# Row parts for three tiles at a time on VectorE, and another pace of the row fetches before and after the first gates

## The chip, the core and the metric

The kernel runs on one core of a Trainium2 chip, as one launch. The metric is device time in microseconds of that launch, lower is better. The core has a matrix engine (PE in the rows, TensorE), a vector engine (DVE), a scalar engine (ACT), GpSimd (POOL), a queue engine (SP) and 16 DMA engines that all transfers share.

## What is computed

A decoder trunk of two layers over 256 positions of width 1024. Each layer has a mixer and then an expert-retrieval stage, `peer`, with 16,384 experts:

```
def peer(xn, w_q, sub_keys, u, v):
    q = (t @ w_q).reshape(n_tok, 8, 2, 128)            # 8 heads, two half keys
    sc = einsum('thpd,hpnd->thpn', q, sub_keys)         # scores against 2 x 128 keys
    ... top 16 of each half, top 16 of their sums -> expert numbers e, gate g = softmax
    hid = gelu(einsum('td,thkd->thk', t, u[e]))         # one dot product an expert
    return einsum('thk,thkd->td', g * hid, v[e])
```

All tensors are float32. The whole is: mixer 0 (attention and retention), peer 0, mixer 1 (a short convolution), peer 1, a last norm.

## The kernel before

**Two ways through the experts.** Of the 256 tokens, 96 fetch the rows of `u` and `v` that they chose, and the other 160 (`TD`) are done densely: every expert's `u` row and `v` row is multiplied with all 160 tokens, and the gates (mostly zero) pick. For the 96, one *row step* fetches 128 rows of 1024 floats (0.524 MB, one indirect DMA that GpSimd issues, L866) and reduces them on DVE, L876 for `u` and L891 for `v`. There are 192 row steps a layer: 96 of `u`, then 96 of `v`. Six buffers (`grow`, `rows`) hold fetched rows; a fetch is issued when the step six before it is done.

**The u stage** (`for i in range(NK)`, 128 tiles of `u`, each 128x1024 floats, 0.524 MB, sent by SP). `dense_u` multiplies tile i into a PSUM tile `hid` (8 products, L1235), ACT applies Gelu into row i of `HG`. Meanwhile DVE works off `pump`, a list of top-16 searches. When it is empty, tile 58, the gates start: `onehots(g)` makes for four tokens two one-hot matrices in the buffer `KO` (8 ACT steps, one DVE step L1190), and `slot`, called twice a tile, adds `rate` to a credit and, at 1, emits `g_mm` (4 products, L1198), `onehots(g+2)` and `g_put`, which multiplies the gates into `HG` (L1208). There are 40 such groups. `ga.rate` says how many row steps are emitted for each tile: 0.6 up to tile 7, 0.88 from there to the gates, then so many that `UPTO[l]` steps are done by tile 117.

**The v stage** (128 tiles of `v`, sent by SP and ACT in turn, eight buffers `raw`). 33 tiles are multiplied as they are (L1324). The 95 *split* tiles (`SPL`: every odd one and every fourth, so that there is one whole tile, then three split ones) are cut into a high part `vhi` (ACT, L1246) and a low part `vlo` (DVE, L1253). The 160 numbers of `HG` that belong to the tile are cut likewise: `hs` holds the high part (ACT, L1300) and the rest (GpSimd, L1305), and `hb` a bf16 copy (ACT, L1301). PE then does eight products of `vhi` with both halves of `hs` (L1328) and eight of `vlo` with `hb` (L1330). At tile i, the parts of tile i+3 are made, the rests of tile i+2, and the DMA of tile i+7 is issued. The other row steps are spread over tiles 2 to 114.

**Order.** Every engine runs its instructions in the order in which the program emits them; a wait holds what is behind it on that engine.

Of the kernel before, what the change touches and what calls it, by code (L numbers as in the profile page):

```python
# [18 lines left out]
P = 128  # L19
# [21 lines left out]
MORE = 4  # L41
GT = 4
SCR = 11 * D
UPTO = (126, 119)
SPL = [i for i in range(NK) if i % 2 or i % 4 == 0 and i > 0]
CODE = 64.0
WHOLE = 1.5 * 2.0 ** 23
# [135 lines left out]
def trunk_kernel(ctx, tc, x, small, cst, mcst, ew_in, ew_out, ow_in, ow_out, wq, keys, pu, pv, pun, gains, out):  # L183
# [33 lines left out]
    KO = pers.tile([P, NPAIR * NK], F32, tag="ko", name="ko")  # L217
# [21 lines left out]
    def nm(s):  # L239
        uid[0] += 1  # L240
        return f"{s}{uid[0]}"
# [250 lines left out]
    class Final(Sums):  # L492


        def __init__(self, xs, g):
            super().__init__()
            self.xs = xs
            self.g = g

        def warm(self):  # L500
# [66 lines left out]
    def split_act(c2, cb, k, src, t, alone=False):  # L567
# [345 lines left out]
    def peer(l, before, norm):  # L913
        with tc.tile_pool(name=nm("hg"), bufs=1) as hp:
# [7 lines left out]
                assert off[0] <= NK * TD  # L922
                return flat[:, o:o + n]

            skT = KO
# [330 lines left out]
            for i in range(NK):  # L1256
                ps = dense_u(i)
                if i == 0:
                    after_first()
                elif early_u:  # L1260
                    fetch(early_u.pop(0))
                if i == NK - 1:
                    gst["rate"] = 1.0
                    while gst["g"] < NG:
                        slot(i)
                T = max(gst["g"], 0) * GT
                if T < TD:
                    act.activation(HG[:, i, T:], ps[:, T:TD], AF.Gelu)  # L1268
                if T > 0:
                    act.activation(ps[:, :T], ps[:, :T], AF.Gelu)  # L1270
                    v.tensor_tensor(HG[:, i, :T], ps[:, :T], HG[:, i, :T], OP.mult)  # L1271
                slot(i + 1)
                if gst["g"] < 0:
                    if i == first_late - 2:
                        pump.flush()
                    if pump.q:
                        pump.run(1.4)
                    else:
                        gst["g"] = 0
                        gst["rate"] = NG / (2.0 * (NK - 8 - i))  # L1280
                        onehots(0)
                        onehots(1)
                ga.rate = (0.6 if i < 8 else 0.88) if gst["g"] < 0 else (UPTO[l] - ga.c) / (NK - CALM - i) if i < NK - CALM else 0.6
                if i < NK - QUIET:
                    ga.step()
                elif i in (NK - QUIET, NK - QUIET + 2):
                    weight_parts(i - NK + QUIET + 1)
            upool.close()
            vpool = ExitStack()
            vp = vpool.enter_context(tc.tile_pool(name=nm("vp"), bufs=3))  # L1290
            OT = XG.rearrange("p q d -> p (q d)")[:, :ND * S].rearrange("p (b t) -> p b t", b=ND)

            assert ga.c >= STEPS
            ga.rate = (ga.TOTAL - ga.c) / (NK - 14.0)
            vo = [acc_tile(b, nm("vo")) for b in range(4)]
            vo += [side_tile(nm("vo")) for _ in range(2)] + [hid_tile(nm("vo")) for _ in range(2)]
            def row_parts(j):
                hsb[j] = hs, hb = [vp.tile([P, 2, TD], F32R, tag="hs", name=nm("hs")),
                                   vp.tile([P, TD], BF16, tag="hb", name=nm("hb"))]
                act.copy(hs[:, 0, :], HG[:, j, :])  # L1300
                act.copy(hb, HG[:, j, :])  # L1301

            def row_rest(j):
                hs = hsb[j][0]
                gp.tensor_tensor(hs[:, 1, :], HG[:, j, :], hs[:, 0, :].bitcast(F32), OP.subtract)  # L1305

            for j in (1, 3):
                row_parts(j)
                row_rest(j)
            for i in range(NK):  # L1310
                j = i + AHEAD
                if 4 <= j and j in SPL:
                    weight_parts(j, False)
                    row_parts(j)
                if 4 <= j - 1 and j - 1 in SPL:
                    weight_rest(j - 1)
                    row_rest(j - 1)
                if i == NK - 8:
                    norm.warm()
                w = st.next()  # L1320
                m = dict(start=i == 0, skip_group_check=True)
                if i not in SPL:
                    for b in range(ND):
                        pe.matmul(vo[b][:, :TD], w[:, b * P:(b + 1) * P], HG[:, i, :], stop=False, **m)  # L1324
                else:
                    hi, lo, (hs, hb) = whi.pop(i), wlo.pop(i), hsb.pop(i)
                    for b in range(ND):
# [25 lines left out]
    with tc.manual_schedule():  # L1353
        norms = [Norm(0)]
        nc.sync.dma_start(G, small)
        nc.sync.dma_start(C[:, :P], cst[:, :P])
        for th in range(2):
            (nc.scalar if th else nc.sync).dma_start(h[:, th, :], x[th])
        nc.sync.dma_start(C[:, P:], cst[:, P:])
        v.memset(Z, 0.0)  # L1360
        act.activation(norms[0].w[:, 0, 6:7], Z[:, 0:1], AF.Sqrt)
        for _ in range(3):
            st._load()
        busy(24)
# [7 lines left out]
        peer(1, a, Final(KO.rearrange("p (a d) -> p a d", a=2), XF.rearrange("p k t -> p (k t)")[:, :D]))  # L1372


# [36 lines left out]
```

## Time and profile before

| | |
|---|---|
| time, median of 3 runs | 1518.8 us (1514.49 to 1521.89) |
| the profiled execution's own time | 1520.15 us |
| its span, first to last instruction | 1518.4 us |
| PE busy | 1461.4 us, 96% |
| DVE, ACT, POOL busy | 1218.0, 812.0, 891.7 us |
| moved by DMA | 533.05 MB, mean 351 GB/s |

By the times at which the engines change lines, the u stage of layer 0 runs from 183.4 to 508.8 us, its v stage to 764.7, the u stage of layer 1 from 919.5 to 1243.9, its v stage to 1505.6. Shares over the whole span mix these stages with the mixers, so the tables by stage below are what is to be read.

### The profile page before, as it was taken

Reading aid. Unit: us, or ns where it says so; the run is one execution under the profiler, and the core shown is the slowest. Engines: PE = TensorE matmul, PEld = TensorE weight load, DVE = VectorE, ACT = ScalarE, POOL = GpSimd, SP = SyncE. Lnnn points to the kernel's source line nnn. Section 1 sums busy time; section 2 is a strip of 40 time slices with the busy share of each in tenths; the row PEclk is TensorE's granted clock in tenths of the full one; section 3 lists DMA queues with packets and bytes.
Section 4 is the critical chain, followed back from the end, with each engine's and each line's share of the span. In section 5 each row is a group of like instructions: output and inputs, shape, how many; then the busy total and the mean of one; then the engine's idle time right before and its main releaser. Section 6 shows DMA issues by size and latency. Waiting matters only on the chain.

```text
span 1518.4 us, 30875 instructions
## 1 busy us (share of the span) xinstructions
PE 1461.4 (96%) x11108; PEld 1364.2 (90%) x11108; DVE 1218.0 (80%) x2406; ACT 812.0 (53%) x2062; POOL 891.7 (59%) x704
## 2 busy tenths in 40 slices
PE   9999999989999999999999999998999999999997
PEld 5667999989999998889989799998999998988896
DVE  5637999868888788888787599995788869888896
ACT  5556512258887455555653462213888845555554
POOL 6754545445554587778535273553565538787763
PEclk9999999999999999999999999999999999999999
DMA  8546899999999999999966498999999999999993
GB/s 314 196 153 207 288 406 409 397 407 409 407 401 409 390 401 409 395 395 393 337 217 198 150 321 335 409 407 397 385 394 393 392 380 392 408 407 400 403 393 141
DMA packets 147577, 533.05 MB, mean 351 GB/s; under 512 B 16992, under 2 KB 17248, under 8 KB 147424
## 3 DMA queue, kind: packets, MB, share of 16 engines
q1 hardware_dynamic: 72144, 258.36, 45.1%
q0 software_dynamic: 56704, 205.07, 34.5%
q10 hardware_dynamic: 18576, 67.64, 11.7%
q8 instruction: 88, 1.44, 0.4%
q14 instruction: 65, 0.53, 0.1%
HBM read 528.34 MB, written 1.05 MB: 349 GB/s over the span
## 4 chain that ended last, share of the span: by engine, by line
PE 50%; DVE 23%; DMA 18%; issue 4%; POOL 3%; ACT 2%; ACTq 0%; SPq 0%; POOLq 0%; DVEq 0%
PE hid L1235 17%; DMA raw<-pv 13%; PE vo L1328 7%; PE G L1198 4%; PE vo L1324 4%; DMA rows<-pun,ig 4%; DVE rows L876 3%; PE vo L1330 3%; PE hid L250 3%; DVE hg L992 2%; DVE hg L998 2%; DVE hg L994 2%; DVE grow L876 2%; PE ea L286 2%; PE ea L285 2%
## 5 line engine op out<-in xcount | busy, mean ns | idle before, releaser
L1235 PE MATMUL hid<-xf,raw 128*128 128x160 f32 x3456 | 489.6, 300 | 0.0
L1235 PEld LDWEIGHTS hid<-xf,raw 128*128 128x128 f32 x3456 | 476.4, 191 | 0.0
L1246 ACT CAST vhi<-raw 128x1024 fp32r<-128x1024 f32 x190 | 198.9, 1047 | 227.5 <-DMA raw<-pv 155.6
L1253 DVE TENSOR_TENSOR vlo<-raw,vhi 128x1024 bf16<-128x1024 f32 x190 | 246.7, 1303 | 88.6 <-ACT vhi L1246 87.6
L1328 PE MATMUL vo<-hs,vhi 128*128 128x320 f32 x1520 | 272.8, 321 | 23.9 <-POOL hs L1305 23.6
L1328 PEld LDWEIGHTS vo<-hs,vhi 128*128 128x128 f32 x1520 | 226.0, 189 | 31.8 <-POOL hs L1305 31.7
L866 POOL DMA_INDIRECT rows<-pv,ig x128 | 177.2, 1384 | 100.6 <-DVE gacc L891 44.5
L1305 POOL TENSOR_TENSOR hs<-hg,hs 128x160 fp32r<-128x160 f32 x190 | 202.4, 1072 | 51.0 <-ACT hs L1300 47.8
L866 POOL DMA_INDIRECT rows<-pun,ig x128 | 153.8, 1202 | 133.2 <-DVE rows L876 71.8
L146 POOL TENSOR_TENSOR lo<-raw,hi 128x1024 bf16<-128x1024 f32 x68 | 163.2, 2415 | 76.8 <-ACT hi L144 73.8
L876 DVE SCALAR_TENSOR_TENSOR rows<-rows,xg 128x1024 f32<-128x1024 f32 x128 | 155.2, 1218 | 31.5 <-DMA rows<-pun,ig 31.4
L1268 ACT ACTIVATE hg<-hid 128x160 f32<-128x160 f32 (+25 forms) x242 | 63.8, 269 | 214.5 <-PE hid L1235 208.8
L891 DVE SCALAR_TENSOR_TENSOR gacc<-rows,ghid,gacc 128x1024 f32<-128x1024 f32 x124 | 171.5, 1383 | 5.8 <-DMA rows<-pv,ig 5.4
L1324 PE MATMUL vo<-hg,raw 128*128 128x160 f32 x1056 | 157.2, 302 | 0.5 <-DVE hg L1271 0.5
L1324 PEld LDWEIGHTS vo<-hg,raw 128*128 128x128 f32 x1056 | 145.5, 190 | 0.8 <-DVE hg L1271 0.8
L1330 PE MATMUL vo<-hb,vlo 128*128 128x160 bf16 x1520 | 139.1, 235 | 0.0
L1189 ACT ACTIVATE ko<-ko,idxT 128x128 f32<-128x128 f32 x320 | 130.8, 481 | 0.0
L866 POOL DMA_INDIRECT grow<-pun,ig x64 | 75.7, 1183 | 87.9 <-DVE grow L876 52.0
L866 POOL DMA_INDIRECT grow<-pv,ig x64 | 86.7, 1355 | 61.0 <-DVE gacc L891 33.1
L1186 ACT ACTIVATE ko<-cst,idxT 128x128 f32<-128x128 f32 x320 | 102.4, 390 | 33.2 <-PE G L1198 33.0
L1330 PEld LDWEIGHTS <-vlo 128*128 128x128 bf16 x1520 | 101.3, 99 | 19.6 <-issue 0.2
L144 ACT CAST hi<-raw 128x1024 fp32r<-128x1024 f32 x100 | 102.5, 1047 | 18.2 <-issue 10.2
(228 smaller groups left out, 2198.9 us busy)
## 6 DMA issues: line engine op xcount, KB each, us to landing
raw<-pu SPq DMA_DIRECT2D x216, 512.0 KB, 7.6
raw<-pv SPq DMA_DIRECT2D x128, 512.0 KB, 7.8
raw<-pv ACTq DMA_DIRECT2D x128, 512.0 KB, 7.8
raw<-wq SPq DMA_DIRECT2D x32, 512.0 KB, 3.9
raw<-ew_in SPq DMA_DIRECT2D x28, 512.0 KB, 4.5
raw<-ow_in SPq DMA_DIRECT2D x24, 512.0 KB, 5.3
hg<-pu SPq DMA_DIRECT2D x22, 512.0 KB, 5.2
raw<-ew_out SPq DMA_DIRECT2D x8, 512.0 KB, 3.2
```

Source lines behind the costliest of these rows:

```text
L146: eng.tensor_tensor(lo, t, hi.bitcast(F32), OP.subtract)
L866: gp.indirect_dma_start(self.row(s_), None, table, bass.IndirectOffsetOnAxis(IG[:, 0, s_ % STEPS:s_ % STEPS + 1].bitcast(U32), 0))
L876: v.scalar_tensor_tensor(r, r, 1.0, XG[:, q % 2, :], op0=OP.mult, op1=OP.mult, accum_out=w)
L891: v.scalar_tensor_tensor(self.acc[q], r, w, self.acc[q], op0=OP.mult, op1=OP.add)
L1189: act.activation(B[:, j], B[:, j], AF.Relu, bias=idxT[:, 2, t:t + 1], scale=idxT[:, 3, t:t + 1])
L1235: pe.matmul(ps[:, :TD], w[k], XF[:, k, :], start=k == 0, stop=k == ND - 1)
L1246: act.copy(whi[j], raw)
L1253: v.tensor_tensor(wlo[j], raw, whi[j].bitcast(F32), OP.subtract)
L1305: gp.tensor_tensor(hs[:, 1, :], HG[:, j, :], hs[:, 0, :].bitcast(F32), OP.subtract)
L1324: pe.matmul(vo[b][:, :TD], w[:, b * P:(b + 1) * P], HG[:, i, :], stop=False, **m)
L1328: pe.matmul(vo[b][:, :2 * TD], hi[:, b * P:(b + 1) * P], hs, stop=i == NK - 1, **m)
L1330: pe.matmul(vo[b][:, :TD], lo[:, b * P:(b + 1) * P], hb, stop=i == NK - 1, **m)
```

## The change

The rest of a row part, `hs[:, 1, :]`, is made by DVE, for a whole run of split tiles (three, at the ends one) in one instruction, and ACT makes the high parts and the bf16 copies of a run in one instruction each. The two halves of the key buffer `KO`, free once the gates are done, hold `hs` in turn. So GpSimd keeps only the row fetches in the v stage. Three tables of numbers change: `UPTO` of layer 1, the row rate ahead of the gates (0.9 for tiles 8 to 45, then 0.6), and the pace of the gates, which begins at a credit of -0.6 and ends two tiles earlier.

```diff
-UPTO = (126, 119)
+UPTO = (126, 122)
...
                         gst["g"] = 0
-                        gst["rate"] = NG / (2.0 * (NK - 8 - i))
+                        gst["rate"] = NG / (2.0 * (NK - 10 - i))
+                        gst["credit"] = -0.6
...
-                ga.rate = (0.6 if i < 8 else 0.88) if gst["g"] < 0 else (UPTO[l] - ga.c) / (NK - CALM - i) if i < NK - CALM else 0.6
+                ga.rate = (0.9 if 8 <= i < 46 else 0.6) if gst["g"] < 0 else (UPTO[l] - ga.c) / (NK - CALM - i) if i < NK - CALM else 0.6
...
+            halves = new_ko(F32R).rearrange("p (a n) -> p a n", a=2)[:, :, :6 * TD]
...
             def row_parts(j):
-                hsb[j] = hs, hb = [vp.tile([P, 2, TD], F32R, tag="hs", name=nm("hs")),
-                                   vp.tile([P, TD], BF16, tag="hb", name=nm("hb"))]
-                act.copy(hs[:, 0, :], HG[:, j, :])
-                act.copy(hb, HG[:, j, :])
-
-            def row_rest(j):
-                hs = hsb[j][0]
-                gp.tensor_tensor(hs[:, 1, :], HG[:, j, :], hs[:, 0, :].bitcast(F32), OP.subtract)
+                n = run_of(j)
+                hs = halves[:, (j + 1) // 4 % 2].rearrange("p (j s t) -> p j s t", j=3, s=2)[:, :n]
+                hb = vp.tile([P, 3, TD], BF16, tag="hb", name=nm("hb"))[:, :n]
+                act.copy(hs[:, :, 0, :], HG[:, j:j + n, :])
+                act.copy(hb, HG[:, j:j + n, :])
...
+            def row_rest():
+                j, n, hs = hsb.pop("rest")
+                v.tensor_tensor(hs[:, :, 1, :], HG[:, j:j + n, :], hs[:, :, 0, :].bitcast(F32), OP.subtract)
...
                 if 4 <= j and j in SPL:
                     weight_parts(j, False)
-                    row_parts(j)
+                    if j - 1 not in SPL:
+                        row_parts(j)
                 if 4 <= j - 1 and j - 1 in SPL:
                     weight_rest(j - 1)
-                    row_rest(j - 1)
+                    if "rest" in hsb:
+                        row_rest()
```

DVE's instructions in layer 0, u stage, around the first one-hots (`ko<-cst,idxT`); the rows L876 (L882) are row steps. Before:

```order
L1103 TENSOR_TENSOR hg_1256<-hg_1256 128x128
L876 SCALAR_TENSOR_TENSOR rows_2048,ghid_1261<-rows_2048,xg 128x1024 x2
L876 SCALAR_TENSOR_TENSOR grow_1257,ghid_1261<-grow_1257,xg 128x1024 x2
L876 SCALAR_TENSOR_TENSOR rows_2048,ghid_1261<-rows_2048,xg 128x1024 x4
L1190 TENSOR_TENSOR ko<-cst,idxT_1265 128x512 x2
L876 SCALAR_TENSOR_TENSOR grow_1257,ghid_1261<-grow_1257,xg 128x1024 x2
L876 SCALAR_TENSOR_TENSOR rows_2048,ghid_1261<-rows_2048,xg 128x1024
L1190 TENSOR_TENSOR ko<-cst,idxT_1265 128x512
```

and after:

```order
L1109 TENSOR_TENSOR hg_1256<-hg_1256 128x128
L882 SCALAR_TENSOR_TENSOR rows_2048,ghid_1261<-rows_2048,xg 128x1024 x2
L882 SCALAR_TENSOR_TENSOR grow_1257,ghid_1261<-grow_1257,xg 128x1024 x2
L882 SCALAR_TENSOR_TENSOR rows_2048,ghid_1261<-rows_2048,xg 128x1024 x2
L1196 TENSOR_TENSOR ko_612<-cst,idxT_1265 128x512 x2
L882 SCALAR_TENSOR_TENSOR rows_2048,ghid_1261<-rows_2048,xg 128x1024 x2
L882 SCALAR_TENSOR_TENSOR grow_1257,ghid_1261<-grow_1257,xg 128x1024 x2
L1196 TENSOR_TENSOR ko_612<-cst,idxT_1265 128x512
```

Two row steps fewer stand ahead of the first two one-hots, and four instead of three between them and the third.

PE at the same place, with the tiles `hid` of the u stage and the first two gate groups `G`. Before:

```order
L1235 MATMUL hid_3089<-xf,raw_2947 128x160 x8
L1235 MATMUL hid_3103<-xf,raw_2961 128x160 x8
L1198 MATMUL G_3113<-ko 128x128 x4
L1235 MATMUL hid_3133<-xf,raw_2975 128x160 x8
L1235 MATMUL hid_3151<-xf,raw_2989 128x160 x4
L1198 MATMUL G_3156<-ko 128x128 x4
```

and after:

```order
L1241 MATMUL hid_3083<-xf,raw_2945 128x160 x8
L1241 MATMUL hid_3097<-xf,raw_2959 128x160 x8
L1241 MATMUL hid_3113<-xf,raw_2973 128x160 x4
L1204 MATMUL G_3118<-ko_612 128x128 x4
L1241 MATMUL hid_3113<-xf,raw_2973 128x160 x4
L1241 MATMUL hid_3145<-xf,raw_2985 128x160 x8
L1204 MATMUL G_3157<-ko_612 128x128 x4
```

The first gate group stands half a u tile later.

DVE in the v stage of layer 0, where `vlo` is the low part of a tile and `gacc` a row step. Before:

```order
L1253 TENSOR_TENSOR vlo_5567<-raw_5460,vhi_5546 128x1024
L891 SCALAR_TENSOR_TENSOR gacc_1259<-rows_2048,ghid_1261,gacc_1259 128x1024
L1253 TENSOR_TENSOR vlo_5620<-raw_5499,vhi_5588 128x1024
L1253 TENSOR_TENSOR vlo_5647<-raw_5528,vhi_5614 128x1024
L891 SCALAR_TENSOR_TENSOR gacc_1259<-rows_2048,ghid_1261,gacc_1259 128x1024
```

and after:

```order
L897 SCALAR_TENSOR_TENSOR gacc_1259<-grow_1257,ghid_1261,gacc_1259 128x1024
L1259 TENSOR_TENSOR vlo_5442<-raw_5336,vhi_5415 128x1024
L1326 TENSOR_TENSOR ko_4833<-hg_1256,ko_4833 128x3x160
L1259 TENSOR_TENSOR vlo_5465<-raw_5359,vhi_5440 128x1024
L897 SCALAR_TENSOR_TENSOR gacc_1259<-grow_1257,ghid_1261,gacc_1259 128x1024
```

Once in four tiles DVE now makes the rests of a run, behind the low part of the run's first tile.

## Rows read from the trace of the kernel before

**Rows 1.** Page, GB/s moved in each of 40 equal slices of the span.

```profile
GB/s 314 196 153 207 288 406 409 397 407 409 407 401 409 390 401 409 395 395 393 337 217 198 150 321 335 409 407 397 385 394 393 392 380 392 408 407 400 403 393 141
```

**Rows 2.** Windows, layer 0: stretch, its us, busy by engine, clock, DMA share, GB/s.

```profile
292.00:323.00 31.00, 25.46 (x187) 24.98 (x185) 15.75 (x28) 10.79 (x36) 11.25 (x12) 0.97 1.03 406
331.00:490.00 159.00, 157.83 (x1211) 157.19 (x1210) 136.04 (x251) 130.35 (x448) 88.39 (x75) 1.00 1.02 406
490.00:555.00 65.00, 63.94 (x515) 61.66 (x514) 49.55 (x52) 31.05 (x69) 41.08 (x34) 1.00 1.02 393
555.00:715.00 160.00, 150.84 (x1254) 141.36 (x1253) 134.26 (x104) 86.61 (x177) 127.23 (x106) 1.00 1.02 398
715.00:765.00 50.00, 49.69 (x425) 47.54 (x424) 38.85 (x31) 29.38 (x61) 25.32 (x21) 1.00 0.97 347
```

**Rows 3.** Windows, layer 1 (PE, PEld, DVE, ACT, POOL busy, clock, DMA, GB/s).

```profile
1060.00:1070.00 10.00, 9.87 (x58) 9.90 (x59) 8.01 (x15) 6.73 (x20) 5.20 (x5) 0.75 1.03 402
1070.00:1230.00 160.00, 160.00 (x1234) 160.00 (x1233) 129.69 (x247) 129.44 (x447) 92.54 (x70) 1.00 1.01 392
1230.00:1260.00 30.00, 30.00 (x237) 29.49 (x236) 19.90 (x22) 13.38 (x31) 14.61 (x12) 1.00 0.97 358
1260.00:1460.00 200.00, 186.51 (x1537) 174.98 (x1536) 172.48 (x132) 105.10 (x216) 158.89 (x133) 0.99 1.03 404
```

**Rows 4.** Timeline of PE at the first gates of each layer: start, us, what.

```profile
323.49 2.05 PE L1198 MATMUL G<-ko 128*128 128x128 f32 x8 [5.91 <-DVE ko L1190]
...
1060.13 2.05 PE L1198 MATMUL G<-ko 128*128 128x128 f32 x8 [6.36 <-DVE ko L1190]
...
1066.72 1.05 PE L1198 MATMUL G<-ko 128*128 128x128 f32 x8
...
1070.87 1.05 PE L1198 MATMUL G<-ko 128*128 128x128 f32 x8
```

**Rows 5.** Timeline of DVE ahead of the first one-hots, layer 0.

```profile
318.96 1.23 DVE L876 SCALAR_TENSOR_TENSOR rows<-rows,xg 128x1024 f32<-128x1024 f32 x1 [1.34 <-DMA rows<-pun,ig]
...
321.51 1.23 DVE L876 SCALAR_TENSOR_TENSOR rows<-rows,xg 128x1024 f32<-128x1024 f32 x1 [1.32 <-DMA rows<-pun,ig]
...
322.66 1.29 DVE L1190 TENSOR_TENSOR ko<-cst,idxT 128x512 f32<-128x512 f32 x2
```

**Rows 6.** Timeline of PE, v stage of layer 0, two whole tiles four apart.

```profile
513.54 2.38 PE L1324 MATMUL vo<-hg,raw 128*128 128x160 f32 x16
...
521.05 2.38 PE L1324 MATMUL vo<-hg,raw 128*128 128x160 f32 x16
```

**Rows 7.** The chain that ended last, v stage of layer 0: start, us, what.

```profile
561.15 8.65 DMA raw<-pv
...
677.15 7.70 DMA raw<-pv
```

**Rows 8.** Waits within 505 to 765 and within 1243 to 1506: total us, times, longest.

```profile
PE vo L1328 <- POOL hs L1305: 9.5, 15, 1.7
...
PE vo L1328 <- POOL hs L1305: 14.1, 16, 2.1
```

**Rows 9.** Groups by line, first the whole span, then 505 to 765: busy us, mean ns.

```profile
L1190 DVE TENSOR_TENSOR ko<-cst,idxT 128x512 f32<-128x512 f32 x80 | 54.6, 684 | 0.0
...
L1253 DVE TENSOR_TENSOR vlo<-raw,vhi 128x1024 bf16<-128x1024 f32 x95 | 120.6, 1273 | 48.1 <-ACT vhi L1246 47.5
...
L1305 POOL TENSOR_TENSOR hs<-hg,hs 128x160 fp32r<-128x160 f32 x95 | 108.6, 1149 | 25.5 <-ACT hs L1300 23.8
...
L891 DVE SCALAR_TENSOR_TENSOR gacc<-rows,ghid,gacc 128x1024 f32<-128x1024 f32 x41 | 60.0, 1463 | 0.1
```

**Rows 10.** Timeline of DVE, v stage of layer 0, one beside no GpSimd subtraction, one beside.

```profile
531.93 1.27 DVE L891 SCALAR_TENSOR_TENSOR gacc<-rows,ghid,gacc 128x1024 f32<-128x1024 f32 x1
...
535.89 1.55 DVE L891 SCALAR_TENSOR_TENSOR gacc<-rows,ghid,gacc 128x1024 f32<-128x1024 f32 x1
...
749.20 1.23 DVE L1253 TENSOR_TENSOR vlo<-raw,vhi 128x1024 bf16<-128x1024 f32 x1 [3.49 <-ACT vhi L1246]
```

More of the change, by code (lines that the diff above doesn't have):

```diff
@@ L216, in trunk_kernel @@
     G = pers.tile([P, 7 * ND], F32, tag="small", name="small")
-    KO = pers.tile([P, NPAIR * NK], F32, tag="ko", name="ko")
     ident = C[:, C_ID:C_ID + P]
@@ L492, in trunk_kernel, with __init__ @@
     class Final(Sums):
-        def __init__(self, xs, g):
+        def __init__(self, g):
             super().__init__()
-            self.xs = xs
             self.g = g
@@ L511, in done @@
         def done(self, a, junk):
+            if a == 0:
+                self.xs = new_ko().rearrange("p (a d) -> p a d", a=2)
             self.square(a, junk)
@@ L574, in split_act, with new_ko @@
             gp.tensor_copy(cb[:, k, t], c2[:, k, 0, t].bitcast(F32))
+    def new_ko(dtype=F32):
+        xv["ko"] = pers.tile([P, NPAIR * NK], dtype, tag="ko", name=nm("ko"))
+        return xv["ko"]
     def load_keys(l):
+        KO = new_ko()
         for c in (slice(0, 4 * NK), slice(4 * NK, NPAIR * NK)):
@@ L923, in scr @@
                 return flat[:, o:o + n]
-            skT = KO
+            KO = skT = xv["ko"]
             qT = [scr(S) for _ in range(2)]
@@ L1289, in peer @@
             vpool = ExitStack()
-            vp = vpool.enter_context(tc.tile_pool(name=nm("vp"), bufs=3))
+            vp = vpool.enter_context(tc.tile_pool(name=nm("vp"), bufs=2))
             OT = XG.rearrange("p q d -> p (q d)")[:, :ND * S].rearrange("p (b t) -> p b t", b=ND)
@@ L1296, in peer, with run_of @@
             vo += [side_tile(nm("vo")) for _ in range(2)] + [hid_tile(nm("vo")) for _ in range(2)]
-            def row_parts(j):
-                hsb[j] = hs, hb = [vp.tile([P, 2, TD], F32R, tag="hs", name=nm("hs")),
-                                   vp.tile([P, TD], BF16, tag="hb", name=nm("hb"))]
-                act.copy(hs[:, 0, :], HG[:, j, :])
-                act.copy(hb, HG[:, j, :])
-            def row_rest(j):
-                hs = hsb[j][0]
-                gp.tensor_tensor(hs[:, 1, :], HG[:, j, :], hs[:, 0, :].bitcast(F32), OP.subtract)
+            halves = new_ko(F32R).rearrange("p (a n) -> p a n", a=2)[:, :, :6 * TD]
+            def run_of(j):
+                n = 1
+                while j + n in SPL:
+                    n += 1
+                return n
+            def row_parts(j):
+                n = run_of(j)
[3 more added lines that the diff above has]
+                act.copy(hb, HG[:, j:j + n, :])
+                for a in range(n):
+                    hsb[j + a] = hs[:, a], hb[:, a]
+                hsb["rest"] = j, n, hs
+            def row_rest():
+                j, n, hs = hsb.pop("rest")
+                v.tensor_tensor(hs[:, :, 1, :], HG[:, j:j + n, :], hs[:, :, 0, :].bitcast(F32), OP.subtract)
             for j in (1, 3):
                 row_parts(j)
-                row_rest(j)
+                row_rest()
             for i in range(NK):
@@ L1313, in peer @@
                     weight_parts(j, False)
-                    row_parts(j)
+                    if j - 1 not in SPL:
+                        row_parts(j)
                 if 4 <= j - 1 and j - 1 in SPL:
                     weight_rest(j - 1)
-                    row_rest(j - 1)
+                    if "rest" in hsb:
+                        row_rest()
                 if i == NK - 8:
@@ L1371, in trunk_kernel @@
         odd_mixer(b, a)
-        peer(1, a, Final(KO.rearrange("p (a d) -> p a d", a=2), XF.rearrange("p k t -> p (k t)")[:, :D]))
+        peer(1, a, Final(XF.rearrange("p k t -> p (k t)")[:, :D]))
 def kernel(**inputs):
```

## The prediction

> **What bounds the kernel now.** I read the GB/s by slice first, then windows by stage, then the waits inside them. From slice 6 to 19 and 26 to 39, the two `peer` stages, the DMA engines move about 400 GB/s, and no slice passes 409 [rows 1]. One tile of `u` or `v`, and one row step, is 0.524 MB, so 0.524 / 0.409 = 1.28 us of DMA each. PE is full or nearly so in the same stretches [rows 2, 3]. So two resources stand level, and the question of each saved wait on PE is whether DMA has room to follow.
>
> PE has these losses. (a) At the first gates it idles 5.91 and 6.36 us for the one-hots on DVE [rows 4]. TensorE's granted clock then falls to the lower level, 1.2 GHz, for part of a stretch that averages 0.75 [rows 3]: from the first gate group to the second 1066.72 - 1060.13 = 6.59 us, to the third 4.15 [rows 4], so 2.4 us more. (b) In the v stages PE waits 9.5 and 14.1 us for `hs` [rows 8]. (c) What else it loses is small: 1.2 of 159 us behind the gates of layer 0 [rows 2].
>
> Why are the one-hots late? DVE works in order, and ahead of them stand row steps that wait for their rows: one every 321.51 - 318.96 = 2.55 us [rows 5]. That is 2 x 1.28: the fetched rows get half of the DMA, the `u` tiles the other. In that stretch DMA moves 406 GB/s while PE idles [rows 2]. So the 6 us on PE are no 6 us of DMA.
>
> The v stage, layer 0: four tiles take PE 521.05 - 513.54 = 7.51 us [rows 6]. On the chain stand fifteen landings of `raw` in a row, from 561.15 to 684.85 [rows 7]; the load of tile j+4 is issued behind the cut of tile j on ACT, so a piece is four tiles, 8.25 us. DMA needs for four tiles and 2.2 row steps (62 steps over 114 tiles) 6.2 x 1.28 = 7.9 us; in layer 1 (69 steps, 2.4) 8.2. So up to about tile 103, where the last row is asked for, DMA is ahead of PE as the limit, and what remains (50 us at 347 GB/s, PE 49.69) is PE's alone [rows 2].
>
> **The change part by part.**
>
> *First gates.* The order of DVE shows two row steps fewer ahead of the first one-hots: they are ready 2 x 2.55 = 5.1 us sooner. PE reaches the first group half a tile later: three half tiles and a group of equal size take 4.15 us, so about 1.04. Layer 0: ready at 322.66 + 0.68 - 5.1 = 318.2, wanted at 323.49 - 5.91 + 1.04 = 318.6. Layer 1: the same step ends the wait at 1060.13 - 5.1 = 1055.0, wanted at 1060.13 - 6.36 + 1.04 = 1054.8. So the first wait goes to about 0. What is late next: between these one-hots and the third stand four row steps instead of three; at 2.55 us they end at 318.2 + 10.2 + 0.7 = 329.1, and PE wants the third group two groups on, at 318.6 + 8.3 = 326.9. I expect 2.2 us there, too short for the clock to fall, seeing that the gaps it fell after were about 6 us. PE's gain: 5.91 + 2.4 - 2.2 = 6.1 in layer 0, 6.36 + 2.4 - 2.2 = 6.6 in layer 1, sum 12.7. Bounds: 17.1 if the third group waits for nothing, 0 if the old wait only moves there.
>
> *Row rates after the gates.* Layer 0 asks for 79 instead of 76 steps up to tile 117, layer 1 for 75 instead of 69: 3.8 and 7.7 us of DMA more in that stage. Three of the steps in layer 1 leave the v stage, whose DMA need falls by 3 x 1.28 = 3.8 us. Gate groups come 3% denser; DVE has 136.04 of 159 us there [rows 2], which covers it.
>
> *Row parts on DVE.* Per layer, GpSimd loses 95 subtractions (108.6 us in layer 0 [rows 9]) and DVE gets 31 of 480 numbers and two of 160. No row has a fp32 subtraction of 480; a DVE step of 512 takes 0.684 [rows 9], a low part of 1024 takes 1.23 undisturbed [rows 10], so between 0.58 and 0.68; I take 0.64, as the 512 row is nearest: 31 x 0.64 + 2 x 0.25 = 20.3 us per layer. It gives some back. A row step takes 1.55 beside a GpSimd subtraction and 1.27 without [rows 10], 1.463 in the mean [rows 9]; a low part 1.273 in the mean and 1.23 alone. Without the subtractions: 41 x 0.19 + 95 x 0.043 = 12 us. Net DVE is 8 us busier per layer, of which 160 / 256 falls in the stretch with 134.26 of 160 us [rows 2], which becomes 139: hidden, as long as the idle time left is not in the wrong place. ACT (86.61 of 160) does fewer, longer copies: nothing. GpSimd keeps only row fetches, so PE's waits on it, 23.6 us, lose their last link; the `raw` landing behind most of them stays.
>
> The Trainium skill, in Perfetto Trace Analysis, Optimizing Scalar/DVE Operations, says that GpSimd and DVE share an SBUF read port, so that shifting work between them might not help. The trace agrees on the sharing (1.55 against 1.27), and by that rule the shift itself would be worth nothing, the sum 8.7 instead of 12.1.
>
> *`KO` and queues.* The one-hots are done by tile 121, the halves are written after tile 127, and the keys of the next layer and the last norm come after the last product: no wait. No load moves in SP's queue.
>
> **The sum goes by DMA.** All bytes stay. From the gates to tile 103 of v, the end can move only by DMA time that idles today: (409 - GB/s) / 409 x us. Layer 0: 1.2 (331 to 490), 2.5 (490 to 555), 4.3 (555 to 715) [rows 2]. Layer 1: 6.7 (1070 to 1230), 3.7 (1230 to 1260), 2.4 (1260 to 1460) [rows 3]. Together 20.8. What of it is won is my choice:
> - u, layer 0: 0; it stands at 406 and the demand only grows.
> - u, layer 1: its demand grows by 7.7, more than its idle 6.7; it should stand like layer 0, which left 1.2 idle. Won: 5.5.
> - u to v: earlier arrival with fewer tiles in store keeps the queues filled. Half: 1.3 and 1.9.
> - v: dips come where GpSimd issued rows late, behind `hs`. Half: 2.2 and 1.2.
>
> Sum 12.1, of which 3.4 (the two v halves) hang on GpSimd; PE's own savings (12.7 and a part of 23.6) are larger, so DMA is the tighter limit. The profiled execution took 1520.15 (span 1518.4 and 1.75 around it), so 1508.05; it lies 1.35 above the median of three runs (1518.8), from which I forecast 1506.7, say **1507**. Runs of one kernel differ by up to 0.5% (1514.49 to 1521.89), about what a measurement can tell from no change; that is 7.6 us.
>
> **Rivals.**
>
> *Given back in v.* DMA is saturated in both v stages, so PE arrives sooner, finds fewer tiles in store and waits for `raw` instead. Only the three steps that find idle DMA in u of layer 1 count: 1518.8 - 3.8 = 1515. For it: 8.25 us a piece against 7.51 [rows 6, 7]; against: 392, 358 and 393 GB/s where it idles.
>
> *The gate wait only moves.* The third group waits long enough for the clock to fall again: 2.4 us of the gain lost in each layer. PE then keeps 12.7 - 4.8 = 7.9 and something of 23.6; in layer 1 that cuts what DMA can be given: 1518.8 - 12.1 + 4.8 = 1511.5.
>
> *DMA is no limit.* All of PE's waits go: 1518.8 - 12.7 - 23.6 - 3.8 = 1479. Against it every GB/s row.
>
> *Slower: DVE late in v.* The run's subtraction stands behind the run's first low part and ahead of the next ones and of the row steps. DVE's 48.1 us of waiting for `vhi` [rows 9] follow the landings, so they needn't shrink when work is added. If none of the 20.3 us fits into them and nothing is given back, low parts come later, `raw` buffers free later, and both v stages stretch: 1518.8 + 40.6 - 12.7 - 3.8 = 1543. It decides from DVE needing more than a piece's 8.25 us: it needs three low parts, 2.2 row steps and one rest, 3 x 1.273 + 2.2 x 1.463 + 0.64 = 7.7, so it takes more than 0.5 of forced waiting per four tiles.
> The Trainium skill, in the same section, says: "If Scalar/Vector aren't saturated, but are causing bubbles on other engines, breaking up instructions may allow work to be completed sooner." Here instructions are merged; by that rule this rival would be the outcome. No row of before shows a merged one.
>
> **How the numbers follow.** Forecast 0.55 (its own range 1499 to 1511), given back 0.22, gate wait moves 0.10, no limit 0.05, DVE late 0.08. Faster by over 7.6 us: 0.55 + 0.05 + half of the gate case 0.05, and a little of the first rival, 0.67. Same: 0.25. Slower: 0.08. The range leaves out the last two rivals: below, all idle DMA used, 1518.8 - 20.8 = 1498, and 2 for a low run; above, given back with DVE's step at its dear end, 1521.
>
> **What will show it.** First gates: the wait behind `G` under 1 us, a shorter one at the third group, the clock at 2.4 GHz throughout. Layer 1, 1070 to 1230: over 400 GB/s. v stages: no PE wait on GpSimd, landings of `raw` still on the chain at about 8 us a piece. Rests on DVE near 0.64, row steps near 1.3, low parts near 1.23. Wrong I am if DMA runs unsaturated in v while DVE is over 95% busy there (slower), or if both u stages lose their wait and the end doesn't move (given back).

## The result, and the profile after

The changed kernel takes 1506.65 us (median of five runs, 1505.18 to 1508.67), the kernel before 1518.67 beside it (five runs, 1514.49 to 1521.89). The ratio is 0.9928, 95% interval 0.9906 to 0.995. The interval leaves out 1, so the changed kernel is faster, by about 0.7%. The profiled execution took 1506.65 us, its span is 1504.9.

Where the time went is read from six stages of the profiled executions. A u stage goes from its first product to the first of the v stage behind it, a v stage to the end of its last product. In us:

| kernel | start | u, layer 0 | v, layer 0 | between | u, layer 1 | v, layer 1 |
|---|---|---|---|---|---|---|
| before | 183.3 | 325.5 | 255.9 | 154.9 | 324.4 | 261.6 |
| after | 182.2 | 324.9 | 253.7 | 154.9 | 319.1 | 257.2 |
| difference | -1.1 | -0.6 | -2.2 | 0.0 | -5.3 | -4.4 |

Behind the last v stage stand 12.8 us in both. How far a stage differs between two profiles of the same kernel shows in the changed kernel's second profile (`after_again`, below): u 324.5 and 318.7, v 253.8 and 258.4, so by up to 0.4 us in u and 1.2 in v. The same windows as in [rows 2] and [rows 3], now of the changed kernel: stretch, its us, busy us (and count) of PE, PE's weight load, DVE, ACT, POOL, granted clock, DMA share, GB/s. First layer 0, then layer 1.

```profile
292.00:323.00 31.00, 29.48 (x219) 29.49 (x220) 16.28 (x29) 14.42 (x46) 11.34 (x12) 1.00 1.03 408
331.00:490.00 159.00, 153.28 (x1172) 151.93 (x1171) 135.90 (x248) 125.21 (x433) 94.77 (x75) 1.00 1.02 406
490.00:555.00 65.00, 63.56 (x517) 61.58 (x516) 50.09 (x58) 27.90 (x42) 21.87 (x17) 1.00 1.02 393
555.00:715.00 160.00, 153.53 (x1282) 144.46 (x1281) 134.95 (x124) 80.26 (x100) 60.87 (x45) 1.00 1.02 405
```

```profile
1060.00:1070.00 10.00, 9.78 (x76) 9.57 (x75) 8.11 (x19) 8.16 (x28) 4.45 (x4) 1.00 1.03 409
1070.00:1230.00 160.00, 159.33 (x1222) 158.69 (x1221) 134.87 (x250) 123.05 (x422) 89.26 (x73) 1.00 1.02 405
1230.00:1260.00 30.00, 29.08 (x237) 28.02 (x236) 23.14 (x25) 13.86 (x21) 8.94 (x7) 1.00 1.02 394
1260.00:1460.00 200.00, 190.69 (x1580) 178.06 (x1578) 169.06 (x156) 99.63 (x124) 75.53 (x55) 1.00 1.03 406
```

Read the last column against that of before: 398 has become 405 in v of layer 0, 392 has become 405 in u of layer 1, 358 has become 394 between them, and 406 and 393 in layer 0 have stayed. Most of the time was won in stages where GB/s rose. The exception is v of layer 1: it is 4.4 us shorter at 406 where it was 404, but it has three row steps fewer, 3.8 us of DMA. In the second row PE is busy for 153.28 us where it was 157.83, while DMA moves the same 406: PE has more time to spare there than before, and the stage is no shorter for it.

The first gates, the rows that answer to [rows 4] and [rows 5]. First PE in layer 0 (start, us, engine, line, operation, tiles; in brackets the idle time ahead and who ended it), then PE in layer 1, then DVE in layer 0.

```profile
319.27 1.05 PE L1204 MATMUL G<-ko 128*128 128x128 f32 x8
323.42 1.05 PE L1204 MATMUL G<-ko 128*128 128x128 f32 x8
327.79 1.13 PE L1204 MATMUL G<-ko 128*128 128x128 f32 x8
...
337.61 1.13 PE L1204 MATMUL G<-ko 128*128 128x128 f32 x8 [1.28 <-DVE ko L1196]
```

```profile
1052.78 1.05 PE L1204 MATMUL G<-ko 128*128 128x128 f32 x8
```

```profile
315.57 1.23 DVE L882 SCALAR_TENSOR_TENSOR rows<-rows,xg 128x1024 f32<-128x1024 f32 x1 [1.31 <-DMA rows<-pun,ig]
316.72 1.29 DVE L1196 TENSOR_TENSOR ko<-cst,idxT 128x512 f32<-128x512 f32 x2
318.14 1.23 DVE L882 SCALAR_TENSOR_TENSOR rows<-rows,xg 128x1024 f32<-128x1024 f32 x1
...
326.96 0.69 DVE L1196 TENSOR_TENSOR ko<-cst,idxT 128x512 f32<-128x512 f32 x1
```

The waits of 5.91 and 6.36 us are gone, and a group now takes 1.05 us at once where the first took 2.05: in this profile the granted clock stays at 2.4 GHz (1.00 in every window above, where [rows 3] had 0.75). But look at what PE waits for in 200 to 505 us as a whole (total, times, longest), before and then after:

```profile
PE G L1198 <- DVE ko L1190: 7.1, 4, 5.9
```

```profile
PE G L1204 <- DVE ko L1196: 5.7, 6, 1.4
```

One long wait has become six short ones, of not much smaller a sum, and u of layer 0 is 0.6 us shorter.

In the v stages the answers to [rows 9] and [rows 10] (groups by line, 505 to 765 us, layer 0: busy us, mean ns, then idle ahead):

```profile
L1259 DVE TENSOR_TENSOR vlo<-raw,vhi 128x1024 bf16<-128x1024 f32 x95 | 115.6, 1222 | 46.3 <-ACT vhi L1252 38.2 <-PE vo L1353 4.7 <-PE vo L1351 1.4
...
L897 DVE SCALAR_TENSOR_TENSOR gacc<-rows,ghid,gacc 128x1024 f32<-128x1024 f32 x41 | 52.3, 1274 | 0.0
...
L897 DVE SCALAR_TENSOR_TENSOR gacc<-grow,ghid,gacc 128x1024 f32<-128x1024 f32 x20 | 25.6, 1279 | 0.1
L1326 DVE TENSOR_TENSOR ko<-hg,ko 128x480 fp32r<-128x480 f32 (+1 forms) x33 | 20.8, 632 | 0.0
```

The 20 row steps over `grow` stood so before:

```profile
L891 DVE SCALAR_TENSOR_TENSOR gacc<-grow,ghid,gacc 128x1024 f32<-128x1024 f32 x20 | 29.8, 1492 | 0.0
```

The row steps fell from 1463 and 1492 to 1274 and 1279 ns and the low parts from 1273 to 1222: with GpSimd's subtractions gone DVE gets back 7.7 + 4.2 + 5.0 = 16.9 us of the 20.8 that it took over. Over the whole v stage of layer 0 its busy time (the third one) is the same before and after. Steps that follow each other at once overlap a little in the records, so groups add up to more than the busy time.

```profile
508.80:764.70 255.90, 245.67 (x2050) 231.76 (x2048) 210.22 (x163) 142.93 (x292) 187.94 (x153) 1.00 1.01 388
```

```profile
507.10:760.80 253.70, 245.11 (x2050) 231.57 (x2048) 210.27 (x196) 130.93 (x168) 78.07 (x58) 1.00 1.01 393
```

PE's waits on GpSimd, 9.5 and 14.1 us [rows 8], are gone; in their place (505 to 765, then 1234 to 1495 us) stand waits for the merged step on DVE:

```profile
PE vo L1351 <- DVE ko L1326: 6.9, 9, 1.4
```

```profile
PE vo L1351 <- DVE ko L1326: 8.2, 12, 1.5
```

And the chain that ended last still runs over the landings of `raw`, as in [rows 7] (start, us, what):

```profile
560.33 7.89 DMA raw<-pv
568.34 9.50 DMA raw<-pv
```

### The profile page after: what moved, and what is told of

It reads as the page before. It is cut to its first block, busy times and chain, and to the rows that moved or that the text cites. A ratio compares the mean times of both kernels' runs of the same rounds, so it can differ in the third digit from the quotient of the medians.

```text
span 1504.9 us, 30131 instructions
## 1 busy us (share of the span) xinstructions
PE 1457.2 (97%) x11108; PEld 1358.3 (90%) x11108; DVE 1214.9 (81%) x2472; ACT 786.3 (52%) x1812; POOL 678.8 (45%) x514
## 3 DMA queue, kind: packets, MB, share of 16 engines
HBM read 528.34 MB, written 1.05 MB: 352 GB/s over the span
## 4 chain that ended last, share of the span: by engine, by line
PE 36%; DMA 33%; DVE 20%; issue 6%; ACT 2%; POOL 2%; ACTq 0%; DVEq 0%; SPq 0%; POOLq 0%
DMA raw<-pv 20%; PE hid L1241 9%; DMA rows<-pun,ig 8%; PE vo L1351 6%; DMA grow<-pv,ig 3%; DVE rows L882 3%; PE vo L1347 3%; PE hid L249 3%; PE vo L1353 2%; PE G L1204 2%; DVE hg L998 2%; DVE hg L1000 2%; DVE hg L1004 2%; DMA grow<-pun,ig 2%; PE ea L285 2%
## 5 line engine op out<-in xcount | busy, mean ns | idle before, releaser
L1259 DVE TENSOR_TENSOR vlo<-raw,vhi 128x1024 bf16<-128x1024 f32 x190 | 231.4, 1223 | 89.2 <-ACT vhi L1252 74.3
L1351 PE MATMUL vo<-ko,vhi 128*128 128x320 f32 x1520 | 270.7, 320 | 16.5 <-DVE ko L1326 15.1
L872 POOL DMA_INDIRECT rows<-pv,ig x128 | 167.7, 1310 | 237.5 <-DVE gacc L897 194.4
L1351 PEld LDWEIGHTS vo<-ko,vhi 128*128 128x128 f32 x1520 | 224.6, 188 | 24.8 <-DVE ko L1326 23.1
L882 DVE SCALAR_TENSOR_TENSOR rows<-rows,xg 128x1024 f32<-128x1024 f32 x128 | 155.6, 1220 | 43.4 <-DMA rows<-pun,ig 35.3
L1274 ACT ACTIVATE hg<-hid 128x160 f32<-128x160 f32 (+14 forms) x240 | 62.9, 269 | 200.9 <-PE hid L1241 165.0
L897 DVE SCALAR_TENSOR_TENSOR gacc<-rows,ghid,gacc 128x1024 f32<-128x1024 f32 x124 | 158.4, 1277 | 9.7 <-issue 4.5
L249 PE MATMUL hid<-x,hi 128*128 128x256 f32 x800 | 107.4, 287 | 2.0 <-DVE cg L818 1.3
```

The lines of the kernel that those rows point to most:

```text
L249: pe.matmul(ps[:, :S], hi[:, k * P:(k + 1) * P], A2[:, k, s_, :], start=k == 0 and s_ == 0, stop=False)
L872: gp.indirect_dma_start(self.row(s_), None, table, bass.IndirectOffsetOnAxis(IG[:, 0, s_ % STEPS:s_ % STEPS + 1].bitcast(U32), 0))
L882: v.scalar_tensor_tensor(r, r, 1.0, XG[:, q % 2, :], op0=OP.mult, op1=OP.mult, accum_out=w)
L897: v.scalar_tensor_tensor(self.acc[q], r, w, self.acc[q], op0=OP.mult, op1=OP.add)
L1259: v.tensor_tensor(wlo[j], raw, whi[j].bitcast(F32), OP.subtract)
```

## The experiments

Theory A is the prediction's: the end moves by DMA time that idled, PE's own savings are larger than that, and the v stages' part comes from GpSimd. Its rivals: B, the gain is GpSimd set free in v; C, PE's waits at the gates are worth what they measure; and for the v part, that the engine doesn't matter and the merging does. Each ratio is to the kernel before, run beside it.

**The numbers alone.** Before, with the three tables of numbers from the change and the row parts left on GpSimd.

```diff
-UPTO = (126, 119)
+UPTO = (126, 122)
-gst["rate"] = NG / (2.0 * (NK - 8 - i))
+gst["rate"] = NG / (2.0 * (NK - 10 - i))
+gst["credit"] = -0.6
-ga.rate = (0.6 if i < 8 else 0.88) if gst["g"] < 0 else ...
+ga.rate = (0.9 if 8 <= i < 46 else 0.6) if gst["g"] < 0 else ...
```

> The kernel before with the three tables of numbers of the change (row rates, pace of the gates, UPTO), and the row parts as they were. Theory A (the end moves only by DMA time that idled before): the u stage of layer 1 and its passage to v gain 7 to 8 us, the v stage of layer 0 nothing; 1509 to 1513 us. The first wait for the one-hots is gone in both layers, and in layer 0 the u stage is as long as before (324 to 326 us). Theory B (the gain of the change is GpSimd set free in v): within 3 us of the kernel before, 1516 to 1520. Theory C (PE's wait at the gates was worth what it measured): 17 us, 1501 to 1504.

Measured 1512.7 us, ratio 0.9952 (0.9936 to 0.9969). The stages: u of layer 1 319.1, as in the whole change; u of layer 0 324.5. So all of the gain in the u stages comes from the numbers. The v stages, 254.5 and 259.1, are 1.4 and 2.5 us shorter than before, and PE waits for GpSimd in them about as before (8.6 and 12.6 us).

**The parts alone.** The changed kernel with the old numbers.

> The changed kernel with the old tables of numbers: only the row parts are made for runs of three on VectorE. Theory A: only the dips of DMA in the v stages are won, 2 to 5 us; 1514 to 1517, and the first wait for the one-hots stays at 5 to 7 us with the clock halved behind it. Theory B: nearly the whole gain, 1506 to 1510.

1514.18 us, 0.9966 (0.9956 to 0.9976). u of layer 1 stays at 323.4, v is 253.1 and 259.3. The two halves gain 0.0048 and 0.0034 apart, the whole 0.0072: two causes, the one mostly in u of layer 1, the other in v, and their sum, 0.0082, is the whole within the intervals. In the v stages each half shows some of the gain. u of layer 0 is 324.9 here, with the first gate's wait in it, and 324.9 in the whole change, without.

**DMA made free: half the tiles' bytes.** In both kernels the tiles of u from 72 on and all tiles of v load only their left half, and the halves are used twice, so all instructions stay and the output is another one.

```diff
-(self.nc.scalar if len(src) > 2 and src[2] else self.nc.sync).dma_start(t, src[0])
+n = D // 2 if len(src) > 3 and src[3] else D
+(self.nc.scalar if len(src) > 2 and src[2] else self.nc.sync).dma_start(t[:, :n], src[0][:, :n])
...
```

> The kernel before with DMA set free behind the gates: of the u tiles from 72 on and of all v tiles only the left half is loaded and used twice, so that every engine does the same steps with 0.262 MB instead of 0.524 (the output is another one). Theory A: the waits of the v stages that come from landings go, those at the gates stay: 1486 to 1498; u stages within 2 us of the kernel before, first gate waits of 6 us in both.

> The changed kernel with the same halved loads (the output is another one). Theory A: with DMA out of the way PE's saved gate waits show: the u stage of layer 0, equally long before and after with full loads, is 6 to 9 us shorter than in the same kernel before with halved loads, that of layer 1 too, and the two kernels stand 16 to 25 us apart (1466 to 1478). Rival (what gave the gate wait back is VectorE's order, not DMA): the u stage of layer 0 stays as long, and they stand 12 us apart as with full loads.

1484.93 us, 0.9768 (0.9748 to 0.9788), just under what was expected, and 1469.38 us, 0.9666 (0.9646 to 0.9686), within it. This tells most of all. Window 331 to 490 of the two, columns as above:

```profile
331.00:490.00 159.00, 159.00 (x1226) 159.00 (x1226) 138.90 (x256) 131.38 (x450) 101.67 (x77) 1.00 0.94 335
```

```profile
331.00:490.00 159.00, 159.00 (x1226) 159.00 (x1225) 142.21 (x261) 127.00 (x438) 102.36 (x78) 1.00 0.96 349
```

| kernel | u, layer 0 | v, layer 0 | u, layer 1 | v, layer 1 |
|---|---|---|---|---|
| before, half the bytes | 324.8 | 240.9 | 324.6 | 243.4 |
| after, half the bytes | 317.6 | 241.1 | 317.6 | 241.0 |

With DMA below its limit PE is busy all the time, and the change's numbers save 7.2 and 7.0 us of u. In layer 0 of the real kernel 0.6 of these 7.2 are left, in layer 1 5.3 of the 7.0. Before, u of layer 0 was no shorter with half the bytes (324.8 against 325.5): PE and DMA stood level there, as the prediction read it. And with DMA free the v stages of layer 0 do not differ (0.2 us), those of layer 1 by 2.4 us. The gap between the two kernels is 15.5 us, a little under the span that theory A gave to it; its u part is as large as worked out, its v part smaller.

A second reading goes against the prediction. In the half-byte kernel of before GpSimd subtracts as ever. PE's waits in its v stages: none in layer 0, and in layer 1 (total, times, longest)

```profile
PE vo L1334 <- POOL hs L1311: 1.5, 3, 0.7
```

where they were 9.5 and 14.1 [rows 8]. So with the landings out of the way GpSimd's subtractions hold PE up for 1.5 us in all.

**Seven row steps fewer in u of layer 0.** The changed kernel with `UPTO = (119, 122)`.

> The changed kernel with UPTO of layer 0 at 119 instead of 126: seven row steps go from its u stage to its v stage. Theory A: the u stage is 4 to 6 us shorter, since it waited for rows behind the gates, the v stage 5 to 9 us longer; together 1506 to 1511. Rival (rows in u cost PE, rows in v are hidden): 1500 to 1503.

1508.22 us, 0.9921 (0.99 to 0.9941): no difference from the change. But the stages moved: u of layer 0 from 324.9 to 318.5, v from 253.7 to 260.2. Seven steps at 1.28 us are 9.0 us of DMA; 6.4 left u, and 6.5 came back in v. PE is again busy in the window:

```profile
331.00:490.00 159.00, 158.01 (x1217) 157.80 (x1216) 134.05 (x253) 126.74 (x437) 85.62 (x71) 1.00 1.02 402
```

So PE's saving at the first gates can be had in u, and DMA takes it back in v. The bytes only changed their place.

**Does the engine matter, or the merging?** First the merged step put on GpSimd:

```diff
-v.tensor_tensor(hs[:, :, 1, :], HG[:, j:j + n, :], ...)
+gp.tensor_tensor(hs[:, :, 1, :], HG[:, j:j + n, :], ...)
```

> The changed kernel with the rest of a run made on GpSimd again, still 480 numbers at once. Theory A: DMA is the limit in v, so a busier GpSimd costs only where it issues rows late: 0 to 3 us against the changed kernel, 1506 to 1510. Theory B: what VectorE took over comes back, 1510 to 1514. The long subtraction is expected at 1.5 to 4 us.

Then before with the new numbers and its single subtractions of 160 put on DVE:

```diff
-gp.tensor_tensor(hs[:, 1, :], HG[:, j, :], ...)
+v.tensor_tensor(hs[:, 1, :], HG[:, j, :], ...)
```

> The kernel before with the new tables of numbers and the rest of each single tile (160 numbers) made on VectorE, not merged. Theory A: VectorE has 95 steps of about 0.25 us instead of 31 of 0.64, 4 us more a layer, hidden: 1506 to 1510. Rival (merging is what helps, since the row parts of tiles two and three of a run lie ready before their weights land): 2 to 6 us slower than the changed kernel, 1509 to 1513.

1509.67 us, 0.9934 (0.9917 to 0.9952), and 1512.66 us, 0.9952 (0.9936 to 0.9969); for the second, theory A had 1506 to 1510, the rival 1509 to 1513. With the numbers alone (single, GpSimd) at 0.9952 and the change (merged, DVE) at 0.9928 the table is whole:

| | on GpSimd | on DVE |
|---|---|---|
| single, 160 | 0.9952 | 0.9952 and 0.9954 |
| merged, up to 480 | 0.9934 | 0.9928 and 0.9931 |

The second numbers are the repeats below. The rows differ by 0.0018 to 0.0026, the columns by 0.0006 at most. Each interval reaches 0.0015 to 0.0022 to either side, so a difference between the engines of some 3 us could hide in them; that of the rows is taken up below. Taking the subtractions off GpSimd one by one gained nothing (1512.66 us against 1512.7 with the numbers alone). Each step of merged work on GpSimd (groups by line, whole span: busy us, mean ns):

```profile
L1326 POOL TENSOR_TENSOR ko<-hg,ko 128x480 fp32r<-128x480 f32 (+1 forms) x66 | 107.9, 1636 | 70.4 <-ACT ko L1318 67.0 <-issue 2.5
```

and of single work on DVE (the same view):

```profile
L1306 DVE TENSOR_TENSOR hs<-hg,hs 128x160 fp32r<-128x160 f32 x190 | 60.2, 317 | 0.0
```

**The same two again,** side by side on one chip, since the difference is small.

> The changed kernel once more, beside the three others: 1504 to 1509 us, v stages 252 to 255 and 256 to 259 us.

> The new tables with the rest of each single tile on VectorE, once more, now on the same chip as the changed kernel. If merging is what helps in v: 3 to 8 us slower than it, DMA at 396 to 400 GB/s in the middle of v against 405. If the first look was chance: within 2 us.

1507.89 us, 0.9931 (0.9915 to 0.9946), and 1511.31 us, 0.9954 (0.9939 to 0.997). The sign is the same, 3.4 us. The intervals against the kernel before overlap a little, but set against each other, five of the six merged runs (1506.37 to 1508.49) lie below all six single ones (from 1509.06). So merging gains on DVE; on GpSimd it is likely, from medians 3.0 us apart (1512.7 and 1509.67) whose runs overlap. What "merged" stands for is three things at once: one subtraction for a run, two copies on ACT for a run, and the parts of six tiles in store where three were. The second one's profile is its lowest run, 1509.06 us, and has the clock at 2.4 GHz from u to the end of v in both layers, as the first profile of the change, 1506.65 us; between these two undisturbed profiles lie 2.4 us.

The rate in v follows neither the engine nor, on GpSimd, the merging. 398 GB/s before and 405 in the change were shown above; at 560 to 720 us the numbers alone (single, GpSimd), the parts alone (merged, DVE), single steps on DVE and their repeat have

```profile
560.00:720.00 160.00, 152.48 (x1269) 143.38 (x1269) 136.39 (x105) 87.25 (x179) 130.22 (x105) 1.00 1.03 405
```

```profile
560.00:720.00 160.00, 152.65 (x1275) 143.66 (x1275) 134.04 (x124) 80.11 (x100) 60.89 (x44) 1.00 1.03 405
```

```profile
560.00:720.00 160.00, 152.66 (x1257) 142.18 (x1255) 136.18 (x163) 85.24 (x175) 62.31 (x44) 1.00 1.02 399
```

```profile
560.00:720.00 160.00, 153.14 (x1269) 142.96 (x1268) 136.21 (x163) 86.64 (x178) 63.34 (x45) 1.00 1.02 402
```

405 stands with all of GpSimd's subtractions in place, 399 and 402 (396 to 400 was expected) with none. Merged steps on GpSimd have 397, in a profile that lies 6 us above the median of its kernel.

**What idles behind tile 103 of v.** [rows 2] showed 347 GB/s at 715 to 765 us, behind the last row. If the limit is DMA, rows spread further into the stage should give time back. On the changed kernel:

```diff
-ga.rate = (ga.TOTAL - ga.c) / (NK - 14.0)
+ga.rate = (ga.TOTAL - ga.c) / (NK - 9.0)
```

> The changed kernel with the row steps of v spread up to tile 119 instead of 114. Theory A: four tiles then ask for 6.1 instead of 6.2 tiles of DMA while DMA is the limit, and the stretch behind, where it idles, takes the rest: 2 to 4 us less in each v stage, 1499 to 1503. Rival (the last rows then meet the sums behind the last tile): 1506 to 1510.

1502.39 us, 0.9885 (0.9867 to 0.9904). v is 250.9 and 254.8, 2.8 and 2.4 us less than in the change. It beats both kernels. Further still, with `NK - 4.0`:

> The changed kernel with the row steps of v spread up to tile 124 (114 in it, 119 in the run that was faster). Theory A: another 1 to 3 us a layer less DMA while DMA is the limit: 1496 to 1501. Rival (what the last rows still need behind them, their sums and three small copies, then ends after the last tile): 1502 to 1508.

1502.65 us, 0.9887 (0.9868 to 0.9905): no more. v gives another 1.9 and 1.6, but the stretch behind it grows from 154.9 to 158.5. Its window at the end of v (columns as above), and that of the change:

```profile
750.00:775.00 25.00, 20.87 (x156) 18.65 (x155) 21.20 (x44) 15.02 (x35) 4.04 (x7) 0.93 0.52 182
```

```profile
750.00:775.00 25.00, 23.50 (x185) 20.97 (x184) 20.26 (x42) 15.87 (x36) 3.51 (x6) 1.00 0.57 199
```

PE stands idle for 4.13 instead of 1.50 us, and the granted clock is 0.93 in the mean: from 761.5 us on it was at 1.2 GHz for 3.4 us. In layer 0 the rows show why. DVE, behind the last row steps, waits for a copy before its second sum over `gacc`, and PE waits behind that for `xg`, first in this kernel, then in the change:

```profile
759.09 1.22 DVE L905 TENSOR_TENSOR h<-gacc,h 96x1024 f32<-96x1024 f32 x1 [1.12 <-DMA gacc<-gacc]
```

```profile
760.60 2.09 PE L1368 MATMUL fq<-cst,xg 128*128 128x128 f32 x8 [3.42 <-DVE xg L1363]
```

```profile
761.33 1.95 PE L1368 MATMUL fq<-cst,xg 128*128 128x128 f32 x8 [0.49 <-DVE xg L1363]
```

2.9 of the 3.6 us are this wait, as the rival had it, and the lower clock comes behind it. The run with the numbers alone has 157.7 between the stages, and there too PE had waited, for 2.06 us at the same place, before a stretch of 3.4 us at 1.2 GHz from 766.7; its last rows are not late. Theory A's further gain in v is there (3.5 us in the two stages) and is lost behind it.

**Are PE's waits for the merged step worth anything?** On the kernel with `NK - 9.0`, the merged step and the next run's copies are put ahead of the weight parts in each tile's turn.

```diff
 for i in range(NK):
+    if "rest" in hsb:
+        row_rest()
+    if i > 1 and i + 5 in SPL and i + 4 not in SPL:
+        row_parts(i + 5)
...
-        if j - 1 not in SPL:
-            row_parts(j)
...
-        if "rest" in hsb:
-            row_rest()
```

> Rows up to tile 119, and the row parts of a run made two tiles sooner, ahead of the low part of the tile whose landing they stood behind: PE's waits for the rests of a run (15 us by the profile of the changed kernel) fall under 4. Theory A: the wait passes to the landing of the tile, the time stays within 3 us of the kernel with rows up to tile 119, 1499 to 1504. Rival (the last link decides): 8 to 12 us less, 1490 to 1495.

1501.93 us, 0.9885 (0.9868 to 0.9901): the same. The waits without and with the edit (whole span; the profile with it is the slowest of its five runs, 1505.72 us):

```profile
PE vo L1351 <- DVE ko L1326: 13.2, 21, 1.6
```

```profile
PE vo L1351 <- ACT vhi L1252: 12.8, 17, 1.6
```

They only change their name. Behind `vhi` stands the landing of `raw`. PE idles for about as long, and what it is seen to wait for is whichever link comes last.

## Why the prediction was right, and where not

**The budget by DMA held.** Forecast 1507, measured 1506.65. PE lost two long waits with a stretch at half clock behind each, and 15.1 us of waits on DVE stand where 23.6 on GpSimd were; the time moved by 12. Shown by the half-byte kernels (PE's saving is there in u when DMA is not the limit, and of the gain in v 0 and 2.4 us are left), by the seven steps moved (6.4 out, 6.5 back) and by the later rows (4.3 us from DMA time that idled). That the sum comes within 0.4 us is in part luck: the halves in it were a choice, single terms were off by up to 1.3 us, and runs of one kernel lie 3.5 us apart.

**First gates: right in the main, missed at the third group.** 6.1 and 6.6 us for PE were worked out; 7.2 and 7.0 were seen with DMA free. The 2.2 us at the third group didn't come in the change, which has no wait there. Its one-hots were ready at 326.96 + 0.69 = 327.65, not at 329.1: the first of the four rows had landed, and the four steps took 8.8 us (318.14 to 326.96) instead of 4 x 2.55. That such a wait would have been too short for the clock to fall was not put to the test there; in the run with the numbers alone it fell after one of 2.06 us. The fifth group waited 1.28 us instead: DVE's lateness was there, and spread. The wait for one-hots sums to 5.7 us against 7.1; it is gone with half the bytes and 1.0 us with seven row steps fewer, so it is DMA's: rows arrive at its pace, and PE waits for as much as it runs ahead.

**u of layer 0:** forecast 0, measured 0.6. **u of layer 1:** forecast 5.5, measured 5.3 (window 1070 to 1230: (405 - 392) / 409 x 160 = 5.1). The first is hardly more than two profiles of one kernel differ by (0.4), and the run with the numbers alone puts the second down to them. What answers to the forecast 5.5 is the 5.1 of the window, idle DMA time; the stage's length is another quantity, since three row steps (3.8 us of DMA) moved into it from v. Over both stages of layer 1 the terms come to 8.6, the windows to 8.7, the stages to 9.7. Without v's halves the sum was 8.7; the numbers alone gained 6.7.

**u to v:** forecast 1.3 and 1.9. Layer 0 won nothing (393 and 393 GB/s), layer 1 (394 - 358) / 409 x 30 = 2.6. Half was a choice: it fitted the sum (3.2 against 2.6), not the layers.

**v: size right, reason wrong.** Forecast 2.2 and 1.2; by GB/s (405 - 398) / 409 x 160 = 2.7 and (406 - 404) / 409 x 200 = 1.0. In layer 1 the stage is 4.4 shorter, of which 3.8 were forecast for the three steps that left. The step that fails is "dips come where GpSimd issued rows late, behind `hs`". With the numbers alone DMA moved 405 and 406 GB/s in these windows with every subtraction on GpSimd, and taking them off GpSimd one by one gained nothing. So the higher rate doesn't need GpSimd set free, and what the parts add to the time comes with the merging. It was in the change's description, and I priced only the shift of engines.

**DVE's prices: right, their sum wrong.** 0.64 us for the merged step against 0.632 in the mean (0.651 for 480 numbers); row steps 1.274, low parts 1.222; only the step of 160 was dearer, 0.317 instead of 0.25. But the prediction took DVE to be 8 us busier per layer, and it is no busier: 210.22 us before and 210.27 after in v of layer 0, 134.26 and 134.95 in the stretch that was to come to 139. What it gets back was counted over 41 row steps and left out the 20 over `grow`. So the shift cost DVE nothing that would have had to be hidden.

The Trainium skill's rule on the shared SBUF read port (Perfetto Trace Analysis, Optimizing Scalar/DVE Operations) fits the time per step, 1463 against 1274 ns, and the end as well: by that rule the shift itself was worth nothing, and the table above shows no difference between engines. The other rule of the Trainium skill's same section that was weighed, that breaking up instructions may let work finish sooner, didn't hold here: the merged step of 480 gave 0.9931, three steps of 160 on the same engine 0.9954.

**Rivals.** "The gate wait only moves" is half true: the sum of the waits stayed in layer 0, but no clock fell in that profile, and it cost nothing that DMA would not have taken. "Given back in v" is what happens to the bytes moved by `UPTO` (119, 122). "DVE late in v" didn't come: DVE waits 38.2 us for `vhi`, so it has room. "No DMA limit" needed half the bytes, and then gave 1469.

**Open.** Why merging helps by some 3 us: putting the steps earlier didn't change the time, so it isn't when PE gets its rests. Rarer stretches at the lower clock are not it: over six runs each on one chip the mean granted clock is 0.995 to 0.997 with merged steps and 0.996 to 0.998 with single ones. DMA's rate in v goes with the merging on DVE (405 and 406 with it, 399 and 402 without), but not on GpSimd (397 and 405). In the profiles of the repeats, 1.6 us apart, the v stages are 1.4 and 0.9 us shorter with merged steps. A run that merges only the copies on ACT, or only the subtraction, was not made.

## What to carry to other kernels

Where two resources stand level, price a change by the idle time of the one that you don't touch: here some 36 us of PE's waits and slow products bought 12, because only DMA time that had idled could be won. To find out which limit holds, halve the bytes and leave all instructions in; the stages that get no shorter have another limit. And a wait that PE shows on an engine names the last link, not the cause: the waits on GpSimd, then DVE, then ACT stood mostly for a tile that had not landed; with half the bytes all but 1.5 us of them were gone.

## What the runs showed of the hardware that was not expected

- In the profile of the merged step on GpSimd (1515.89 us, the slowest of its six runs, median 1509.67), PE's granted clock halved four times in the v stages for 3.4 us each; in the change's own profile it never did there, and before it did once, at 1433.6 us. The profile lies 6 us above the median of its kernel, so differences of this size between two single profiles say little; the ratios here go by all runs of a kernel. A second profile of the change (1507.45 us) has one such stretch, at 294.1 us.
- A GpSimd subtraction of 480 numbers a row took 1660 ns in the mean over the whole span, one of 160 in the kernel before 1072: three times the numbers for 1.5 times the time. On DVE it was 652 against 317.
- Ending GpSimd's arithmetic gave DVE 13% on row steps (1463 to 1274 ns) and 4% on low parts (1273 to 1222) in v of layer 0, 9% and 8% in layer 1 (1399 to 1279, 1335 to 1223). With single subtractions on DVE the first pair is 1274 and 1222 too, with merged ones on GpSimd 1528 and 1317.
